# Attention scores of a head's two maps: hi-by-hi products on halves of the array's rows, crossed products in one pass per map

## The chip, the cores and the metric

The kernel runs on one core of a Trainium2 chip, in one launch. The metric is device time in microseconds (us). The kernel before takes 486.52 us, the median of three runs (486.24 to 486.82). Engine names are those of the profile: PE is the matmul engine and PEld its weight loads, DVE, ACT and POOL are the vector, scalar and GpSimd engines, and SP issues most of the DMAs.

## The reference

The layer takes 1,024 tokens of width 1,024, puts 16 learned meta tokens in front, and runs two mixers side by side on one input projection: differential attention with 4 heads, and a gated linear recurrence. Both have a SiLU gate; one output projection, the residual and a final norm follow. The part that matters here is the attention. A head has two maps, each with its own queries and keys of width 64, and the difference of their two softmaxes weighs the values:

```
scores = jnp.einsum('bqhmd,bkhmd->bhmqk', qb, kb).astype(jnp.float32) * scale
mask = cid[s:e, None] >= cid[None, :kend]
scores = jnp.where(mask[None, None, None], scores, -jnp.inf)
p = jax.nn.softmax(scores, axis=-1)
w = p[:, :, 0] - lam * p[:, :, 1]
outs.append(jnp.einsum('bhqk,bkhd->bqhd', w.astype(vb.dtype), vb))
```

Queries are taken in blocks of 128 and see all keys up to the end of their last chunk of 64, so block i (0 to 7) has 16 + 128(i+1) keys.

## The kernel before, in words

All matrix products keep float32 accuracy by splitting: an operand is stored as a high part (hi) and the rest (lo), and a product is summed from hi by hi, hi by lo and lo by hi. The projections do it with three f32 passes. The scores do it in f16: for each of the 8 maps, the scratch tensors `q_d` and `k_d` in DRAM hold 128 rows, rows 0 to 63 the hi part of the 64 features and rows 64 to 127 the lo part.

The program runs through the projections one weight group after the other (x of the recurrence, K, Q, the attention gate, the recurrence's gate), up to about 247 us. `run_group` walks a group's four blocks of eight k-steps and starts, by the table `PL`, the fetching and splitting of the next group's weights. In the last group, the recurrence's gate, each finished block goes to `g_evac`, in which DVE reads it out of PSUM into the tile `gl`; after block number `LK` it also issues the loads of K and of the first query tile on SP's queue.

Then `attend` goes through 32 steps, one head of one query tile each: tiles 3, 7, 6, 5, 4, 2, 1, 0, so that steps 0 to 3 are tile 3, 4 to 7 tile 7, and so on to steps 28 to 31 for tile 0, with four more steps for what still trails. One step holds, in the order in which every engine gets it:

- the transposes of the hi half of the weights of the head three steps back (`trans(0)`, PSUM tile `pt`, copied by ACT into `wT`);
- `scores` of the head's map 0;
- a first third of the step's fill units. These are pieces of other matrix work (V's projection `psv`, the recurrence's part of the output `psol`, the attention's part `psoa`), some six matmuls each; the table `MF` tells for each step how many are due;
- `combine` of the head before: the two maps' exponentials become one weight matrix;
- a second third of the fill, the transposes of the lo half (`trans(1)`), `scores` of map 1, and the rest of the fill;
- `halve`, which splits the weights of the head before into f16 hi and lo, and `weigh`, the product of weights and values of the head four steps back (PSUM tile `O`).

`scores` writes one map's scores into a PSUM buffer `pss`, by two full passes over K: the first has q as stored (hi over lo) against K as stored, which gives hi by hi and lo by lo; the second has q with its halves exchanged (`q[:, 1]`, loaded so by `load_q`), which gives the two crossed products. Then DVE reduces the buffer (it scales, masks, writes the tile `e` and keeps the extreme in `mx`; the profile's CUSTOM_DVE_ANT_0), and ACT takes the exponential. There are two wide buffers `pss` of two banks each, the same two that the projection groups before use for their blocks, in turn; a buffer can be written again when its reader is done. From tile 2 on, where 400 columns or fewer are needed, the two are of one bank.

All instructions pass through one helper line, L77, so the profile's rows tell operations apart by their tiles, not their lines. In DMA rows, L218 is the load of a projection's weights (`wraw`), L774 that of K, L757 a store of the attention gate.

Of the kernel before, what the change touches and what calls it, by code (L numbers as in the profile page):

```python
# [34 lines left out]
G_XL, G_GL, G_Q, G_K, G_GA, G_V = range(6)  # L35
# [63 lines left out]
def hybrid_layer_kernel(ctx: ExitStack, tc: tile.TileContext, xT, x, meta, w6, nwT,  # L99
# [5 lines left out]
    dma = nc.sync.dma_start  # L105
# [26 lines left out]
    def score_banks():  # L132
        if narrow:
            return narrow[0].tile([P, 512], F32, tag="S1", name="pss")
        return two_banks()
# [635 lines left out]
    def load_k():  # L771
        for m in range(0, NMAP, 2):
            kt = slot("K", [P, 2, T], F16, name="kst")
            dma(kt, qk_d[G_K][m:m + 2].rearrange("m p t -> p m t"))  # L774
            K.extend([kt[:, 0, :], kt[:, 1, :]])

    QT = {}
# [23 lines left out]
            load_k()  # L801
            load_q(tiles[0])

    LK = 1


    rsv = cst([P, NT + 1], name="rsv")
# [70 lines left out]
    def scores(i, h, a):  # L878


        d = st[i]
        n, k0, q, m = d["n"], d["k0"], QT[i], 2 * h + a
        ps = score_banks()
        for j in range(2):
            for s0 in range(0, n - k0, 512):
                s1 = min(s0 + 512, n - k0)
                PE.matmul(ps[:, s0:s1], q[:, j, m, :], K[m][:, k0 + s0:k0 + s1], start=(j == 0), stop=(j == 1))
        e = slot("work", [P, T], name="e")
        mx = d["mx"][:, a, h:h + 1]
        if k0:  # L890
            A.copy(e[:, 0:NM], d["sme"][:, m, :])
        V.tensor_tensor_reduce(out=e[:, k0:n], in0=ps[:, 0:n - k0], in1=mask[:, T - n + k0:], op0=OP.add, op1=OP.min,
                               scale=nesc, scalar=d["m2"][:, m:m + 1] if k0 else -NEG, accum_out=mx)
        if a == 0:
            A.activation(mx, mx, AF.Identity, bias=lnsw)
        A.activation(e[:, 0:n], e[:, 0:n], AF.Exp, scale=-1.0, bias=mx, accum_out=d["sm"][:, a, h:h + 1])
        d["e"][h, a] = e
# [248 lines left out]

    filled = [0]

    MF = [8, 5, 10, 5, 2, 5, 5, 4, 1, 3, 3, 0, 1, 1, 0, 2, 1, 2, 3, 0, 1, 2, 2, 0, 2, 3, 1, 2, 1, 3, 1, 3, 2, 3, 0, 0]

    def at_least(n):
        while fill and filled[0] < n:
# [36 lines left out]
    def attend():  # L1189
# [12 lines left out]
        for s in range(NS + TL + 1):  # L1202
            cur = order[s] if s < NS else None
            com = order[s - 1] if 0 <= s - 1 < NS else None
            tra = order[s - TL] if 0 <= s - TL < NS else None
            filled[0] = 0
            if cur and max(tiles[tiles.index(cur[0]):]) <= PB and not narrow:

                wide.close()
                narrow.append(ctx.enter_context(tc.tile_pool(name="psS1", bufs=NB_[0], space=bass.MemoryType.PSUM)))  # L1210
                narrow.append(ctx.enter_context(tc.tile_pool(name="psF", bufs=NB_[1], space=bass.MemoryType.PSUM)))
            trans(0)
            if cur:
                i, h = cur
                if h == 0:
                    begin(i)
                scores(i, h, 0)
                if h == QH and i in after:
                    load_q(after[i])
            at_least((MF[s] + 2) // 3)  # L1220
            if com:
                combine(*com)
            at_least((2 * MF[s] + 2) // 3)
            trans(1)
            if cur:
                scores(i, h, 1)
                pace()
            at_least(MF[s])
            if com:
                halve(*com)  # L1230
            if avq:
                weigh(*avq[0])
            if tra:
                avq.append(tra)
            while len(backlog) > BL:
                fill_one()
            yield
# [93 lines left out]
```

## Time and profile before

| | |
|---|---|
| median of three runs | 486.52 us |
| the profiled execution | 486.57 us |
| its span, first to last instruction | 484.8 us |
| mean granted PE clock | 0.996 |
| score matmuls (`pss` from `kst` and `qt`) | 208, 247.4 to 442.3 us |
| step 0 starts | 247.4 us |
| the last output products start | 465.3 us |

A PE row of the timeline is a group of matmuls merged, with its start, the time from the first start to the last end, and the count. A matmul's recorded end is modelled and holds its latency, so what one costs in a sequence is read from the distance between starts, not from its length. A weight load (PEld) overlaps the matmul before it. The page's shares of the chain say what the end of the program was waiting for, step by step back from the end. The form 128\*128 before a matmul's shape is rows by columns of the array in use: 16\*128 uses 16 rows.

### The profile page before, as it was taken

What the parts mean: (1) busy time and instruction counts of PE and PEld (TensorE: products, weight loads), DVE (VectorE), ACT (ScalarE), POOL (GpSimd) and SP (SyncE); (2) the same over time, 40 slices, a digit from 0 to 9 for tenths busy, and PEclk for the clock granted to TensorE, in tenths of its full rate; (3) what the DMA queues carried; (4) which work ended last, traced back from release to release, by engine and by line L of the source; (5) the groups of instructions that cost most, each with busy time, mean ns of one, the idle gap of its engine ahead of it and who ended that gap; (6) DMA issues with size and microseconds to landing.
All of it is one profiled execution on the core that took longest, in us unless ns stands there. A gap on an engine that the chain in (4) does not pass through costs nothing.

```text
span 484.8 us, 7748 instructions
## 1 busy us (share of the span) xinstructions
PE 466.2 (96%) x2844; PEld 375.4 (77%) x2844; DVE 364.3 (75%) x610; ACT 303.3 (63%) x592; POOL 126.1 (26%) x171
## 2 busy tenths in 40 slices
PE   6999999999999999999999999999988999999894
PEld 5996989988888888888877577777766778877783
DVE  5756987496799576974574477789999989898443
ACT  5687532663626838441583367698787877797733
POOL 0102202201010000000001044185142425365772
PEclk9999999999999999999999999999999999999998
DMA  7993221344023115239445124953943576315523
GB/s 243 394 398 124 89 89 31 80 121 120 23 65 88 44 43 174 87 124 346 141 139 187 45 61 138 265 172 91 275 110 91 131 193 153 121 32 197 195 88 130
DMA packets 50150, 68.33 MB, mean 141 GB/s; under 512 B 21008, under 2 KB 30128, under 8 KB 50112
## 3 DMA queue, kind: packets, MB, share of 16 engines
q1 hardware_dynamic: 38240, 55.21, 34.6%
q0 software_dynamic: 11872, 12.63, 10.7%
q8 instruction: 22, 0.36, 0.3%
q14 instruction: 16, 0.13, 0.1%
HBM read 48.91 MB, written 18.91 MB: 140 GB/s over the span
## 4 chain that ended last, share of the span: by engine, by line
PE 87%; DVE 5%; ACT 3%; issue 2%; DMA 1%; POOL 0%; POOLq 0%; ACTq 0%; SPq 0%
PE pss L77 42%; PE psv L77 9%; PE psol L77 7%; PE psoa L77 7%; PE ps L77 6%; PE psx L77 5%; PE O L77 4%; DVE e L77 3%; PE psg L77 2%; PE pt L77 2%; DMA res<-res_d 1%; DVE w L77 1%; PE psmr L77 1%; PE pa L77 1%; ACT wT L77 1%
## 5 line engine op out<-in xcount | busy, mean ns | idle before, releaser
L77 PE MATMUL pss<-xs,w 128*128 128x512 f32 (+1 forms) x720 | 142.4, 345 | 4.3 <-ACT xs L77 4.3
L77 PEld LDWEIGHTS pss<-xs,w 128*128 128x128 f32 x720 | 120.4, 190 | 24.5 <-ACT xs L77 4.3
L77 ACT ACTIVATE e<-e,mx 128x528 f32<-128x528 f32 (+7 forms) x64 | 50.5, 790 | 27.4 <-DVE mx L77 26.1
L77 PE MATMUL psv<-w,xs 128*128 128x512 f32 x192 | 48.4, 402 | 0.2 <-DVE v L77 0.2
L77 DVE CUSTOM_DVE_ANT_0 e<-pss,mask,nesc 128x528 f32<-128x528 f32 (+6 forms) x56 | 42.6, 761 | 7.7 <-PE pss L77 6.5
L77 PE MATMUL pss<-w,xs 128*128 128x512 f32 x192 | 46.0, 394 | 0.0
L77 PE MATMUL psol<-woh,lr 128*128 128x512 f32 x128 | 42.8, 415 | 1.9 <-ACT wT L77 1.9
L77 DVE TENSOR_TENSOR w<-wraw,w 128x512 fp32r<-128x512 f32 (+2 forms) x49 | 31.7, 669 | 16.2 <-ACT w L77 16.0
L77 PE MATMUL pss<-kst,qt 128*128 128x512 f16 (+3 forms) x208 | 42.6, 318 | 0.7 <-DVE mx L77 0.7
L77 PEld LDWEIGHTS psv<-w,xs 128*128 128x128 f32 x192 | 35.3, 188 | 10.0 <-issue 0.8
L77 PEld LDWEIGHTS pss<-w,xs 128*128 128x128 f32 x192 | 35.7, 188 | 7.9
L77 PE MATMUL psoa<-woh,at 128*128 128x512 f32 (+1 forms) x136 | 41.6, 389 | 0.2 <-ACT psoa L77 0.2
L77 ACT COPY wT<-pt 128x1024 f16<-128x1024 f16 (+5 forms) x48 | 37.6, 784 | 1.0 <-PE pt L77 0.8
L77 DVE SCALAR_TENSOR_TENSOR e<-e,mx 128x528 f32<-128x528 f32 (+7 forms) x32 | 35.0, 1095 | 1.1
L77 ACT ACTIVATE w<-wraw 128x512 fp32r<-128x512 f32 x47 | 28.5, 619 | 9.7 <-DMA wraw<-in_w_dram 9.2
L77 PE MATMUL ps<-xs,w 128*128 128x512 f32 x120 | 34.4, 394 | 0.0
L77 PEld LDWEIGHTS <-wT 128*128 128x128 f16 x432 | 25.6, 98 | 6.6 <-issue 2.7
L77 PE MATMUL O<-v,wT 128*128 128x128 f16 x432 | 29.4, 219 | 1.3 <-ACT wT L77 1.3
L77 DVE TENSOR_TENSOR w<-e,w 128x528 f16<-128x528 f32 (+7 forms) x32 | 28.9, 904 | 0.9
L77 PEld LDWEIGHTS psol<-woh,lr 128*128 128x128 f32 x128 | 22.9, 188 | 8.6 <-ACT wT L77 3.2
L77 DVE RECIPROCAL a<-a 128x208 f32<-128x208 f32 x20 | 27.8, 1423 | 0.0
L77 PEld LDWEIGHTS psoa<-woh,at 128*128 128x128 f32 x136 | 24.1, 188 | 4.5 <-ACT psoa L77 0.4
(197 smaller groups left out, 838.4 us busy)
## 6 DMA issues: line engine op xcount, KB each, us to landing
wraw<-in_w_dram SPq DMA_DIRECT2D x47, 256.0 KB, 3.9
xt<-in_x_dram SPq DMA_DIRECT2D x8, 512.0 KB, 7.0
woraw<-in_w_out_dram SPq DMA_DIRECT2D x8, 512.0 KB, 3.5
xres<-in_x_dram SPq DMA_DIRECT2D x8, 512.0 KB, 4.9
lr<-lru_d POOLq DMA_DIRECT2D x8, 512.0 KB, 5.1
res_d<-xres SPq DMA_DIRECT2D x8, 512.0 KB, 3.1
res<-res_d SPq DMA_DIRECT2D x8, 512.0 KB, 4.4
out_dram<-res SPq DMA_DIRECT2D x7, 512.0 KB, 2.9
```

Of the source, the lines that this page charges most:

```text
L77: return f(*a, **k)
```

## The change

K is stored differently on the chip: for odd maps the halves are exchanged, lo in rows 0 to 63 and hi in rows 64 to 127. This takes three DMAs for two maps in place of one, twelve in all, and they are issued after block 0 of the last group in place of block 1.

A step writes the scores of both maps at its start. First come hi by hi: map 0 on rows 0 to 63 (hi of q as stored, hi of K) and map 1 on rows 64 to 127 (hi of the exchanged q, hi of the exchanged K), into the two buffers `pss`, in turn for each cut of up to 512 columns. Then each map gets one pass on all rows that adds its two crossed products: map 0 with the exchanged q, map 1 with q as stored against the exchanged K. The product lo by lo, which the first pass held before, is not computed any more. DVE's reduction and ACT's exponential of map 1 follow those of map 0 at once.

Six entries of `MF` change by one, with the same sum.

```diff
@@ load_k
             kt = slot("K", [P, 2, T], F16, name="kst")
-            dma(kt, qk_d[G_K][m:m + 2].rearrange("m p t -> p m t"))
+            dma(kt[:, 0], qk_d[G_K][m])
+
+            dma(kt[0:64, 1], qk_d[G_K][m + 1, 64:128])
+            dma(kt[64:128, 1], qk_d[G_K][m + 1, 0:64])
             K.extend([kt[:, 0, :], kt[:, 1, :]])
...
-    LK = 1
+    LK = 0
@@ scores
-        ps = score_banks()
-        for j in range(2):
-            for s0 in range(0, n - k0, 512):
-                s1 = min(s0 + 512, n - k0)
-                PE.matmul(ps[:, s0:s1], q[:, j, m, :], K[m][:, k0 + s0:k0 + s1], start=(j == 0), stop=(j == 1))
+        cuts = [(s0, min(s0 + 512, n - k0)) for s0 in range(0, n - k0, 512)]
+        if a == 0:
+
+            d["ps"] = [score_banks() for _ in range(2)]
+            for s0, s1 in cuts:
+                for b in range(2):
+                    r = slice(64 * b, 64 * b + 64)
+                    PE.matmul(d["ps"][b][:, s0:s1], q[r, b, m + b, :], K[m + b][r, k0 + s0:k0 + s1], start=True, stop=False)
+        ps = d["ps"][a]
+        for s0, s1 in cuts:
+            PE.matmul(ps[:, s0:s1], q[:, 1 - a, m, :], K[m][:, k0 + s0:k0 + s1], start=False, stop=True)
...
-    MF = [8, 5, 10, 5, 2, 5, 5, 4, 1, 3, 3, 0, 1, 1, 0, 2, 1, 2, 3, 0, 1, 2, 2, 0, 2, 3, 1, 2, 1, 3, 1, 3, 2, 3, 0, 0]
+    MF = [8, 5, 10, 5, 2, 5, 5, 4, 2, 3, 2, 0, 1, 1, 0, 2, 1, 2, 3, 0, 1, 2, 1, 1, 2, 3, 1, 2, 1, 3, 1, 3, 1, 3, 1, 0]
@@ attend
                 scores(i, h, 0)
+                scores(i, h, 1)
+                pace()
                 if h == QH and i in after:
                     load_q(after[i])
...
             trans(1)
-            if cur:
-                scores(i, h, 1)
-                pace()
             at_least(MF[s])
```

The order of instructions at three places. On PE, the start of step 0, from the last matmul of the projection groups on (a number at a tile's name tells its buffers apart, `pss_2090` and `pss_2098` being the last block's). Before:

```order
L77 MATMUL pss_2090<-xs_374,w_1867 128x512
L77 LDWEIGHTS qt_2009
L77 MATMUL pss_2187<-kst_2001,qt_2009 128x512
L77 LDWEIGHTS qt_2009
L77 MATMUL pss_2187<-kst_2001,qt_2009 128x16
L77 LDWEIGHTS qt_2009
L77 MATMUL pss_2187<-kst_2001,qt_2009 128x512
L77 LDWEIGHTS qt_2009
L77 MATMUL pss_2187<-kst_2001,qt_2009 128x16
L77 MATMUL psv_2200<-w_2041,xs_93 128x512
```

With the change:

```order
L77 MATMUL pss_2098<-xs_374,w_1867 128x512
L77 LDWEIGHTS qt_1952
L77 MATMUL pss_2195<-kst_1936,qt_1952 128x512
L77 LDWEIGHTS qt_1952
L77 MATMUL pss_2196<-kst_1936,qt_1952 128x512
L77 LDWEIGHTS qt_1952
L77 MATMUL pss_2195<-kst_1936,qt_1952 128x16
L77 LDWEIGHTS qt_1952
L77 MATMUL pss_2196<-kst_1936,qt_1952 128x16
L77 LDWEIGHTS qt_1952
L77 MATMUL pss_2195<-kst_1936,qt_1952 128x512
```

Two buffers are written in turn from the second score on, where before only one was touched before the V products.

On DVE at the same place, from the reading of the last gate block on (ISA with `e` as output is the reduction of a map's scores). Before:

```order
L77 TENSOR_TENSOR gl<-pss,Rb 128x1024
L77 ISA e,mx_2184<-pss,mask,nesc 128x528
L77 ISA mx_2184 128x1
L77 TENSOR_TENSOR gl<-gl,gls 128x1024
L77 TENSOR_TENSOR gl<-gl,gate_1675 128x1024
L77 TENSOR_TENSOR yl<-gl,yh 128x1024
L77 ISA e,mx_2184<-pss,mask,nesc 128x528
```

With the change:

```order
L77 TENSOR_TENSOR gl<-pss,Rb 128x1024
L77 ISA e,mx_2192<-pss,mask,nesc 128x528
L77 ISA mx_2192 128x1
L77 ISA e,mx_2192<-pss,mask,nesc 128x528
L77 ISA mx_2192 128x1
L77 TENSOR_TENSOR gl<-gl,gls 128x1024
L77 TENSOR_TENSOR gl<-gl,gate_1675 128x1024
```

The second map's reduction stands right behind the first one's, ahead of the gate's products.

On PE in step 34, from the last transposes of tile 0 on. Before:

```order
L77 MATMUL pt<-idh,w_4721 128x128
L77 LDWEIGHTS w_4721
L77 MATMUL pt<-idh,w_4721 128x128
L77 LDWEIGHTS wT
L77 MATMUL O<-v,wT 128x128
```

With the change:

```order
L77 MATMUL pt<-idh,w_4729 128x128
L77 MATMUL psoa<-woh,at 128x512 x2
L77 MATMUL psoa<-wol,at 128x512
L77 MATMUL psoa<-woh,at 128x512 x2
L77 MATMUL psoa<-wol,at 128x512
L77 LDWEIGHTS wT
L77 MATMUL O<-v,wT 128x128
```

One fill unit, six products of the output, now stands between the transposes and the products on `O`.

## The prediction

> **What bounds the kernel now.** I read the page's busy time and chain first, then busy time by stretch, then the timeline of the attention part. The page's lines of busy time and the chain's shares by engine:
>
> ```profile
> span 484.8 us, 7748 instructions
> ...
> PE 466.2 (96%) x2844; PEld 375.4 (77%) x2844; DVE 364.3 (75%) x610; ACT 303.3 (63%) x592; POOL 126.1 (26%) x171
> ...
> PE 87%; DVE 5%; ACT 3%; issue 2%; DMA 1%; POOL 0%; POOLq 0%; ACTq 0%; SPq 0%
> ```
>
> PE is busy 96% of the span and holds 87% of the chain. The change touches only what runs after 247 us. By stretch there (columns: busy us and count of PE, weight load, DVE, ACT, POOL; granted clock; DMA share; GB/s):
>
> ```profile
> 247.00:326.00 79.00, 78.78 (x454) 56.69 (x453) 53.84 (x90) 50.22 (x90) 24.72 (x19) 1.00 0.45 137
> 326.00:400.00 74.00, 68.94 (x653) 53.31 (x651) 70.19 (x126) 59.66 (x129) 26.45 (x37) 1.00 0.58 151
> 400.00:443.00 43.00, 42.65 (x332) 33.97 (x331) 39.19 (x111) 34.96 (x105) 21.89 (x32) 1.00 0.38 111
> 443.00:474.00 31.00, 29.72 (x153) 23.65 (x152) 15.71 (x39) 17.38 (x50) 22.29 (x26) 1.00 0.47 165
> ```
>
> From 247 to 326 (steps 0 to 7: tiles 3 and 7) PE idles 0.2 of 79 us, so each PE microsecond there is one of the kernel. From 326 to 400 (tiles 6, 5, 4) DVE is fuller, 70.2 of 74 against 68.9: both nearly bind, and a PE gain may stay there. From 400 to 474 PE binds again, with 1.6 us idle. After 474 only the last tile's ending is left, which the change leaves alone.
>
> **Fewer passes: -7.9 us.** The score matmuls by shape:
>
> ```profile
> L77 PE MATMUL pss<-kst,qt 128*128 128x512 f16 x96 | 30.3, 380 | 0.0
> ...
> L77 PE MATMUL pss<-kst,qt 128*128 128x400 f16 x32 | 9.2, 332 | 0.7 <-DVE mx L77 0.7
> L77 PE MATMUL pss<-kst,qt 128*128 128x272 f16 x32 | 7.6, 279 | 0.0
> ...
> L77 PE MATMUL pss<-kst,qt 128*128 128x144 f16 x32 | 6.0, 227 | 0.1
> ...
> L77 PE MATMUL pss<-kst,qt 128*128 128x16 f16 x16 | 2.7, 172 | 0.0
> ```
>
> Two pieces of the chain (start, length, instructions), four scores of 512 columns and the product after them:
>
> ```profile
> 295.58 0.86 PE pss L77 x4
> 296.44 0.69 PE psv L77 x3
> ```
>
> The mean of one (380 ns) holds its latency; in a row four take 0.86 us, 0.215 each, or 0.42 ns per column. All scores are 96x512 + 32x400 + 32x272 + 32x144 + 16x16 = 75,520 columns. Before, a head's two maps take four full passes. After, two half-row passes run side by side as one, and two crossed passes follow: three. A quarter of the columns, 18,880 x 0.42 ns = 7.9 us, goes; 2.6 us of it falls in steps 0 to 7, 4.0 between 326 and 400, 1.4 later. If the halves don't run together, this term is 0: these are its two ends. I take the full gain, since the pair reads different rows and writes different PSUM buffers. [...]
>
> **A toll at each change of rows: +5.0 us.** Now every one of the 32 steps goes from 128 rows to 64 and back, 64 changes; the kernel before does it at two small places in the whole program. The nearest rows, three places of PE's timeline:
>
> ```profile
> 256.32 0.64 PE L77 MATMUL pss<-kst,qt 128*128 128x512 f16 x4
> 256.81 1.64 PE L77 MATMUL psv<-w,xs 128*128 128x512 f32 x6
> 258.29 0.28 PE L77 MATMUL psf<-f,ones 128*128 128x8 f32 x2
> 258.43 1.63 PE L77 MATMUL psv<-w,xs 128*128 128x512 f32 x6
> ...
> 276.96 0.64 PE L77 MATMUL pss<-kst,qt 128*128 128x512 f16 x4
> 277.53 0.38 PE L77 MATMUL psvr<-rsv,sl 16*128 16x1 f32 x2
> ...
> 46.23 0.39 PE L77 MATMUL psx<-dgm,ones 16*128 16x16 f32 x2
> 46.55 0.52 PE L77 MATMUL pss<-xs,w 128*128 128x264 f32 x2
> ```
>
> The same four scores are followed after 0.49 us by a product on all rows, after 0.57 by one on 16: 0.08 for going in. A tiny f32 pair on all rows is left after 0.14, the one on 16 rows after 0.32: 0.18, in which slower f32 weight loads are held too. So a change costs from 0 (if halves are not treated so) to 0.18; I take 0.08, the f16 row, since scores are f16. The first one hides in the wait below: 63 x 0.08 = 5.0 us. [...]
>
> **A new wait in step 0: +3.1 us.** The two wide PSUM buffers of the scores are also those of the last two blocks before. The timeline there:
>
> ```profile
> 247.40 0.64 PE L77 MATMUL pss<-kst,qt 128*128 128x512 f16 x4
> ...
> 247.89 8.58 PE L77 MATMUL psv<-w,xs 128*128 128x512 f32 x36
> ...
> 248.71 0.69 DVE L77 TENSOR_TENSOR w<-wraw,w 128x512 fp32r<-128x512 f32 x1 [0.53 <-ACT w L77]
> 249.32 1.22 DVE L77 TENSOR_TENSOR gl<-pss,Rb 128x1024 f32<-128x1024 f32 x1
> 250.46 0.76 DVE L77 CUSTOM_DVE_ANT_0 e<-pss,mask,nesc 128x528 f32<-128x528 f32 x1
> ```
>
> Before, map 0 takes the free buffer at 247.40, and 8.6 us of V products stand ahead of map 1's scores at 256.32; by then DVE has long read the last block of the gate (gl, 249.32 to 250.54) out of the other buffer. Now PE's second instruction of step 0 writes that other buffer. It waits till 250.54, and the 36 V products queued behind it wait too: 250.54 - 247.40 = 3.1 us, with nothing on PE but one half pass. DVE can't be earlier: ahead of gl stand weight splits that wait for ACT. DVE has its two reductions from about 251.4, and the gate's next operations move behind them, by 1.3 us; what they feed is first loaded at 303:
>
> ```profile
> L1040 POOL DMA_DIRECT2D lr<-lru_d x8: 892/948/974, 303.1 to 401.6; - x8
> ```
>
> The bounds are 0 (if DVE came sooner) and 3.3.
>
> **Cover at the end: -1.3 us.** In the last steps PE waits once, for the copy of the last weights:
>
> ```profile
> 452.30 0.33 PE L77 MATMUL O<-v,wT 128*128 128x128 f16 x3
> 452.47 0.22 PE L77 MATMUL ptm<-idh,wm 128*128 128x128 f16 x1
> 453.96 0.34 PE L77 MATMUL O<-v,wT 128*128 128x128 f16 x3 [1.28 <-ACT wT L77]
> ...
> 453.56 0.35 ACT L77 COPY wT<-pt 128x256 f16<-128x256 f16 x1
> ```
>
> The new table moves six output products from step 32 into step 34, between the last transposes and these. Their 1.4 us (six products) cover the 1.28; bounds 0 and 1.3. The table's other moves (one unit each between steps 8 and 10, 22 and 23) keep the count of products and I cost them at 0: they lie in the stretch where DVE binds or swap neighbours. One small wait, V products for DVE in step 1, loses 0.2 since eight scores now stand ahead of it:
>
> ```profile
> 261.56 0.73 PE L77 MATMUL psv<-w,xs 128*128 128x512 f32 x2 [0.22 <-DVE v L77]
> ```
>
> **The K loads: 0.** Twelve DMAs in place of four, issued one block earlier and ahead of two weight loads on SP's queue:
>
> ```profile
> 213.39 0.90 SPq L218 DMA_DIRECT2D wraw<-in_w_dram  x2
> ...
> 214.66 1.96 SPq L774 DMA_DIRECT2D kst<-k_d  x4
> ...
> 222.31 13.15 SPq L218 DMA_DIRECT2D wraw<-in_w_dram  x6
> ...
> 231.31 0.63 ACT L77 ACTIVATE w<-wraw 128x512 fp32r<-128x512 f32 x1
> ```
>
> The page's row of these loads (count, KB, us to landing):
>
> ```profile
> wraw<-in_w_dram SPq DMA_DIRECT2D x47, 256.0 KB, 3.9
> ```
>
> At 0.49 us an issue twelve take 5.9 us, 3.9 more. The two weight loads, issued before at 213.39, now go out at about 225 and land 3.9 us later, against a first use at 231.31. So 2 us of cover are left; without it ACT's splits, and with them gl and the wait above, would slip by what is missing. K itself is first needed at 247.40.
>
> **Map 1's reduction moved up: 0.** DVE now does both reductions of a step, then the combining of the head before, which had to wait for map 1's exponential; that has now a whole step. Queued behind the second reduction are only that combining and the f16 halves, and the transposes that read them come two steps later. In the tight stretch this may win back part of DVE's 3.8 idle us or, if PE comes late to both maps, cost as much; I take 0.
>
> **Sum.** -7.9 + 5.0 + 3.1 - 1.3 - 0.2 = -1.3 us. The profiled execution took 486.57 us (span 484.8 and 1.8 around it), the median is 486.52: 485.3.
>
> **The rivals.**
> 1. *No toll for halves.* Then -6.3; but of the 4.0 us saved between 326 and 400 DVE, with 3.8 idle, lets perhaps half through: 482.3. For it: the tolls shown are of 16 rows and f32 operands, none of 64. Against it: it was paid both in and out.
> 2. *The toll is heavier and eats the gain* (slower). At a change of 0.13, midway between 0.08 and 0.18, 63 changes cost 8.2 us: 488.5. It decides from (7.9 + 1.5 - 3.1) / 63 = 0.10 on. [...] Against it: f16 loads are short.
> 3. *DVE keeps the middle.* What PE saves from 326 to 400, 4.0 less 24 x 0.08 = 2.1 us, only becomes waiting: 487.4. DVE's 70.2 of 74 speaks for it, its 3.8 idle against.
> 4. *The halves don't run together*, so the change doesn't do what it says: +7.9, of which PE's 5.1 idle us in the middle may hide a little: 492.
>
> **How the numbers follow.** My forecast (483.8 to 486.8) gets 0.36, rival 1 0.29, rival 2 0.14, rival 3 0.12, rival 4 0.09. The predicted time is 485.3. The range 480.8 to 489.6 takes in rivals 1 to 3 with their spread and leaves out most of rival 4 and a full gain without toll. About 0.2% (1.0 us) is what a measurement tells from no change. Faster: 0.6 of my forecast and nearly all of rival 1, 0.50. Slower: 0.1 of my forecast, rivals 2 and 4 and half of 3, 0.33. Within 0.2%: 0.17.
>
> **What would show it.** Half-row scores on 64 rows that start in pairs a few tens of ns apart show the passes saved; 0.215 us between the two shows rival 4. The distance from a pair's last matmul to the first crossed one, less its own columns, is the toll. PE idle of about 3 us at 247, ended by DVE's gl, shows the new wait; no idle before the last products on O at about 453 shows the cover. PE's busy time from 326 to 400 falling with DVE's unchanged shows rival 3. I am wrong if step 0 doesn't wait, or if the toll is outside 0 to 0.13.

## The result, and the profile after

The changed kernel takes 491.65 us, the median of three runs (490.58 to 491.92), against 486.52 before. The ratio is 1.010, with a 95% interval from 1.0075 to 1.0125: slower by 1%, where 485.3 us and a small gain had been forecast, and outside the range.

The page of the changed kernel, its span, busy times, chain and the group of the scores:

```profile
span 490.1 us, 7746 instructions
...
PE 466.5 (95%) x2844; PEld 371.5 (76%) x2844; DVE 359.6 (73%) x610; ACT 302.6 (62%) x592; POOL 124.3 (25%) x171
...
PE 73%; DVE 8%; DMA 5%; issue 5%; ACT 5%; POOL 2%; SPq 0%; POOLq 0%; DVEq 0%; ACTq 0%
...
L77 PE MATMUL pss<-kst,qt 64*128 64x512 f16 (+4 forms) x208 | 34.7, 323 | 4.0 <-DVE gl L77 2.7
```

PE is busy as long as before (466.5 us against 466.2), so the saved passes do not show in the sum, and its share of the chain has fallen from 87% to 73%: other engines now hold it up. Busy time by stretch, the columns as in the prediction:

```profile
247.00:251.00 4.00, 1.34 (x7) 0.32 (x6) 2.52 (x3) 2.11 (x6) 0.00 (x0) 0.94 0.30 103
251.00:254.00 3.00, 3.00 (x10) 2.15 (x9) 2.61 (x6) 2.15 (x4) 0.00 (x0) 0.52 0.00 0
247.00:326.00 79.00, 75.63 (x426) 53.92 (x425) 49.80 (x86) 47.01 (x86) 18.60 (x17) 0.98 0.38 114
326.00:400.00 74.00, 67.37 (x644) 49.83 (x643) 65.85 (x118) 57.70 (x118) 30.61 (x38) 1.00 0.61 166
400.00:443.00 43.00, 43.00 (x340) 32.92 (x339) 37.95 (x110) 35.90 (x107) 19.98 (x29) 1.00 0.36 103
443.00:474.00 31.00, 29.43 (x160) 23.19 (x158) 19.04 (x46) 18.06 (x57) 21.29 (x27) 1.00 0.50 174
```

Two things are new. PE idles 3.4 us in the first 79, and from 251 to 254 the granted clock is 0.52 with PE busy all the time. PE's timeline at that place, and DVE's:

```profile
247.26 0.39 PE L77 MATMUL pss<-kst,qt 64*128 64x512 f16 x1
250.31 1.46 PE L77 MATMUL pss<-kst,qt 64*128 64x512 f16 x7 [2.66 <-DVE gl L77]
251.62 6.62 PE L77 MATMUL psv<-w,xs 128*128 128x512 f32 x23
...
249.04 1.22 DVE L77 TENSOR_TENSOR gl<-pss,Rb 128x1024 f32<-128x1024 f32 x1
```

The second score of step 0 comes 3.05 us after the first, released by DVE's `gl`, as forecast. Then three microseconds run at half the clock, which costs 3 x 0.48 = 1.4 us more; that had not been forecast. All that PE waits for from 326 to 400, in the changed kernel (us in total, times, longest), and then before:

```profile
PE pa L77 <- POOL o L77: 2.8, 3, 1.7
PE psol L77 <- ACT wT L77: 1.5, 2, 0.9
PE pss L77 <- DVE mx L77: 1.4, 2, 0.8
PE pt L77 <- DVE mx L77: 1.0, 1, 1.0
```

```profile
PE psol L77 <- ACT wT L77: 1.9, 3, 1.0
PE pa L77 <- POOL o L77: 1.5, 1, 1.5
...
```

6.7 us of waits stand against 5.0 (the three rows left out have 0.7, 0.7 and 0.2): what the array saves there (1.6 us of busy time) is waited away again.

Where the time goes is easiest to see from the start of each step (its first score in the trace), as the difference to the same step before. The table holds some of the runs that are told of below as well; all numbers are us, and "median" is the whole time. A row comes from one execution. The seven kernels with fill first are alike up to step 0, and there their first scores lie up to 0.7 us apart, so a few tenths between two rows mean little.

| kernel | step 1 | 8 | 16 | 20 | 24 | 31 | span | median |
|---|---|---|---|---|---|---|---|---|
| the change | +4.3 | +3.5 | +4.2 | +3.9 | +4.5 | +4.6 | +5.3 | 491.65 |
| fill first (step 0's wait away) | -0.4 | -1.3 | +0.1 | -0.3 | +4.1 | +4.2 | +4.5 | 490.93 |
| the same with the old table | -0.2 | -1.1 | +2.4 | +0.7 | +2.9 | +3.6 | +6.6 | 493.35 |
| new order, full passes, fill first | -0.5 | -0.7 | -1.2 | -2.6 | +2.0 | +1.2 | +5.5 | 492.02 |
| change in steps 0 to 7 alone, fill first | -0.1 | -1.1 | -1.7 | -1.7 | -1.7 | -1.8 | -1.4 | 485.13 |
| the same with step 0's wait | +4.7 | +3.8 | +3.8 | +3.8 | +3.8 | +3.7 | +4.0 | 490.92 |
| change in steps 0 to 19, fill first | 0.0 | -0.9 | -1.0 | -1.0 | +0.2 | -0.5 | +2.4 | 488.74 |
| the same, full passes in steps 8 to 19 | +0.1 | -0.9 | -0.7 | -1.1 | +0.1 | -0.5 | +2.4 | 488.85 |
| the same (halves), old table throughout | -0.1 | -1.1 | +3.7 | +1.9 | +2.6 | +2.6 | +5.7 | 491.72 |

### The profile page after: what moved, and what is told of

The parts are those of the page before. It is cut to its first block, busy times and chain, and to the rows that moved or that the text cites. A ratio compares the mean times of both kernels' runs of the same rounds, so it can differ in the third digit from the quotient of the medians.

```text
span 490.1 us, 7746 instructions
## 1 busy us (share of the span) xinstructions
PE 466.5 (95%) x2844; PEld 371.5 (76%) x2844; DVE 359.6 (73%) x610; ACT 302.6 (62%) x592; POOL 124.3 (25%) x171
## 3 DMA queue, kind: packets, MB, share of 16 engines
q1 hardware_dynamic: 38368, 55.21, 34.7%
## 4 chain that ended last, share of the span: by engine, by line
PE 73%; DVE 8%; DMA 5%; issue 5%; ACT 5%; POOL 2%; SPq 0%; POOLq 0%; DVEq 0%; ACTq 0%
PE pss L77 35%; PE psv L77 9%; PE psoa L77 7%; PE ps L77 6%; PE psol L77 5%; DVE e L77 4%; PE O L77 3%; DMA wraw<-in_w_dram 3%; PE psg L77 2%; PE psx L77 2%; PE pt L77 2%; ACT w L77 2%; DMA xt<-in_x_dram 1%; DVE w L77 1%; DMA res_d<-xres 1%
## 5 line engine op out<-in xcount | busy, mean ns | idle before, releaser
L77 DVE CUSTOM_DVE_ANT_0 e<-pss,mask,nesc 128x528 f32<-128x528 f32 (+6 forms) x56 | 40.6, 763 | 6.2 <-PE pss L77 4.8
L77 PEld LDWEIGHTS psv<-w,xs 128*128 128x128 f32 x192 | 36.4, 193 | 9.8 <-issue 0.8
L77 PE MATMUL pss<-kst,qt 64*128 64x512 f16 (+4 forms) x208 | 34.7, 323 | 4.0 <-DVE gl L77 2.7
L77 ACT ACTIVATE w<-wraw 128x512 fp32r<-128x512 f32 x47 | 28.6, 620 | 10.8 <-DMA wraw<-in_w_dram 10.3
L77 ACT ACTIVATE mx<-mx,lnsw 128x1 f32<-128x1 f32 x32 | 9.4, 295 | 31.0 <-DVE mx L77 30.9
L77 DVE SCALAR_TENSOR_TENSOR e<-e,mx 128x528 f32<-128x528 f32 (+7 forms) x32 | 27.3, 853 | 1.1
```

Source lines behind the costliest of these rows:

```text
L77: return f(*a, **k)
```

## The experiments

Three causes were open: the wait in step 0, the halves with their toll, and the new order (both maps written and reduced at the step's start). Every kernel below computes the whole result.

One thing holds for all of them. The program keeps a model of its own of when each engine is done (`Clock`), and it issues the operations that finish a tile, among them the four transposes `pa` of the attention's output, when the model says that their input is ready. So an edit that shifts the modelled times also moves some of these operations to other places in the queues, and many kernels below differ in more than the edit shown. The pair with halves or full passes in steps 8 to 19 is the cleanest: DVE, ACT and POOL have the same order in both. The kernel with the change in steps 0 to 7 alone and its twin with step 0's wait differ by a few operations of steps 0, 8 and 9 only.

### The wait in step 0 taken away

The wait can go if the other buffer is read before step 0's scores come to it, so three units of fill (V products) are put ahead of them; a second kernel puts one unit there.

```diff
             if cur:
                 i, h = cur
+                if s == 0:
+                    at_least(3)
                 if h == 0:
                     begin(i)
                 scores(i, h, 0)
```

> The changed kernel, but in step 0 the first three fill units (18 V products, 4.2 us by 0.23 each) stand ahead of the scores, so that the last gate block is read before the second buffer is asked for. Theory 1 (the wait at the start of step 0 and the slower clock after it cost 4.3 of the 5.1 us): no PE idle at 247, granted clock 1.00 there, 487.2 us (486.4 to 488.0). Rival (what the changed kernel loses is lost evenly over the steps, by the changes of rows): the gap at 247 goes but the time is won back nowhere, 490 to 491.7.

> As the run with three units ahead, with one unit (6 products, 1.4 us) ahead of the scores: PE still waits about 1.6 us for the buffer. Theory 1 with the clock as a part of its own (waiting 3.05 us costs 3.05, and some 1.4 more as the clock halves for 3 us): the shorter wait leaves the clock at 1.00, 1.6 us above the run with three units, 488.8. Rival (the clock falls after any wait there): 3 us above it, 490.2.

With three units: 490.93 us, ratio to before 1.0085 (1.0068 to 1.0103). With one unit: 492.69 us, 1.0123 (1.0108 to 1.0138), above both expected values. There PE still waits 1.3 us for `gl`, the clock stays at 1.00, and step 1 starts 1.7 us sooner than in the change, but a stall of 2.2 us comes at step 23. In the first, the wait is gone, the clock is not cut there (1.00 from 247 to 262), and at step 8 the kernel is 1.3 us ahead of before and 4.8 us ahead of the change. But at the end only 0.7 us of the 4.8 is left. 4.0 us go in one place, between the starts of steps 22 and 24. PE there, then ACT, then DVE:

```profile
406.94 0.61 PE L77 MATMUL pa<-idf,o 128*128 128x128 f32 x4
409.85 0.49 PE L77 MATMUL pt<-idh,w 128*128 128x128 f16 x6 [2.31 <-ACT wT L77]
...
407.56 0.29 ACT L77 ACTIVATE mx<-mx,lnsw 128x1 f32<-128x1 f32 x1 [1.70 <-DVE mx L77]
407.89 0.63 ACT L77 ACTIVATE e<-e,mx 128x400 f32<-128x400 f32 x1
...
408.52 0.61 ACT L77 ACTIVATE e<-e,mx 128x400 f32<-128x400 f32 x1
...
409.13 0.67 ACT L77 COPY wT<-pt 128x640 f16<-128x640 f16 x1
...
406.40 0.58 DVE L77 TENSOR_TENSOR w<-e,w 128x400 f16<-128x400 f32 x1
406.89 0.63 DVE L77 CUSTOM_DVE_ANT_0 e<-pss,mask,nesc 128x400 f32<-128x400 f32 x1
```

The transposes `pt` wait for a PSUM bank that ACT's copy `wT` empties. The copy now stands behind both exponentials of the step, the first of these waits 1.70 us for DVE's reduction, and DVE comes to that only when it has split the weights of the head before. Before the change one exponential stands there, not two. That alone doesn't make the stall, though. The change has both exponentials ahead of this copy as well, and ACT waits 1.61 us for DVE there (up to 411.31), but PE doesn't wait. What differs is `pa`: `pt`, `ptm` (the transpose of the meta tokens' weights) and `pa` take three banks in turn, so with `pa` ahead the next `pt` needs the bank of the `pt` at 405.75 again. In the change `pa` comes one step later, at 413.88, and a bank is free. The two other kernels with this stall, one unit ahead and the order alone below (2.2 and 3.0 us), have `pa` ahead of it too; no run moves `pa` by itself. After the stall the clock is cut again (0.54, the third number from the end):

```profile
411.00:414.00 3.00, 3.00 (x15) 2.15 (x14) 2.86 (x9) 1.87 (x6) 1.95 (x3) 0.54 0.00 0
```

So the wait in step 0 is real, but taking it away brings a stall elsewhere.

### The table, and the order without halves

Two kernels on the base of fill first: one with the table `MF` of before, one with the new order but two full passes a map (so lo by lo is computed again, as before the change).

```diff
+    MF = [..., 1, 3, 3, 0, ..., 2, 2, 0, 2, ..., 2, 3, 0, 0]   # the old table
```

```diff
-            for s0, s1 in cuts:
-                for b in range(2):
-                    r = slice(64 * b, 64 * b + 64)
-                    PE.matmul(d["ps"][b][:, s0:s1], q[r, b, m + b, :], K[m + b][r, k0 + s0:k0 + s1], start=True, stop=False)
         ps = d["ps"][a]
+        for s0, s1 in cuts:
+            PE.matmul(ps[:, s0:s1], q[:, a, m, :], K[m][:, k0 + s0:k0 + s1], start=True, stop=False)
```

> Three units ahead in step 0, and the table of fill units as it was in the kernel before. If the new table's cover at the end is worth the 1.3 us that I forecast: 1.3 slower than the run with the new table. If its six products only move the wait (the changed kernel still shows 1.9 us of waits for O): within 0.5 us of it.

> Three units ahead in step 0, both maps at the start of a step, but each by two full passes of 128 rows as in the kernel before: no halves, no changes of rows (the product lo by lo is computed again). PE's work in it is 7.9 us more in passes and 6.0 less in changes of rows than with halves, so if PE binds throughout it is 1.9 slower than the run with halves. If the middle (tiles 6, 5, 4) is held by other things than PE, it loses only what steps 0 to 7 and 20 to 31 say: 1.0 slower in the first, 1.0 faster in the last, so the same within 0.5.

The old table: 493.35 us, 1.013 (1.0114 to 1.0145), 2.4 us above fill first. The order alone: 492.02 us, 1.0121 (1.0095 to 1.0148), 5.3 us slower than before without a half pass, a toll or step 0's wait. It is as slow as the change, within the intervals. Its losses lie late: it is 2.6 us ahead of before at step 20, loses 4.6 us by step 24 and 4.3 more behind step 31. So a loss of this size needs no halves; the order makes one, with its table and with the places that `pa` and its like then get. From step 1 to step 8 the halves show their worth: 0.95 us won with them, 0.18 with full passes, so 0.8 us. With the old table one unit less stands in step 8, and a stall of 2.9 us comes in step 9; by step 31 that kernel is level with fill first again, and it loses its 2.4 us behind it (3.0 there, against 0.3).

### The toll, measured by doubling it

The pair and its crossed passes are written cut by cut, so that each of steps 0 to 19, where a map needs two cuts, changes rows four times and not twice.

```diff
             for s0, s1 in cuts:
                 for b in range(2):
                     r = slice(64 * b, 64 * b + 64)
                     PE.matmul(d["ps"][b][:, s0:s1], q[r, b, m + b, :], K[m + b][r, k0 + s0:k0 + s1], start=True, stop=False)
+                for b in range(2):
+                    PE.matmul(d["ps"][b][:, s0:s1], q[:, 1 - b, m + b, :], K[m + b][:, k0 + s0:k0 + s1], start=False, stop=True)
         ps = d["ps"][a]
-        for s0, s1 in cuts:
-            PE.matmul(ps[:, s0:s1], q[:, 1 - a, m, :], K[m][:, k0 + s0:k0 + s1], start=False, stop=True)
```

> Three units ahead in step 0; hi by hi and crossed products of one cut of 512 columns before those of the next, so that every step of tiles 3 to 4 with two cuts (steps 0 to 19) changes rows four times in place of twice. If a change costs 0.095 us (the changed kernel's starts: 0.151 against 0.056 into the pair, 0.308 against 0.215 out of it), each step of tile 7 is 0.2 longer on PE, and by step 8 it is 1.4 to 1.6 us behind the run without (7 steps by 0.2), the whole 1 to 4 slower as far as the middle lets it show. If changes cost nothing, step 8 starts within 0.2 us of that run.

It takes 492.13 us, 1.0116 (1.0101 to 1.0131), 1.2 us above fill first. Up to step 8, where the array sets the time, the sixteen extra changes cost 1.77 us (step 8 starts 0.47 behind before, against 1.30 ahead), 0.11 each. The changed kernel's trace has it directly, at the last step:

```profile
443.21 0.28 PE L77 MATMUL pt<-idh,w 128*128 128x128 f16 x2
443.42 0.47 PE L77 MATMUL pss<-kst,qt 64*128 64x144 f16 x4
443.69 0.71 PE L77 MATMUL psoa<-woh,at 128*128 128x512 f32 x2
```

Two transposes on all rows take 0.11 us in a row; the scores on 64 rows come after 0.21, so 0.10 for going in. The pair and the two crossed passes of 144 columns take 0.06 and 0.12 us; the next product comes after 0.27, so 0.09 for going out.

### Where in the step the second map's work stands

Four kernels keep fill first and the halves and have one edit each. The first puts the crossed pass, reduction and exponential of map 1 back behind the lo transposes, with the new table, and a second the same with the old table. The third leaves the new order and moves the lo transposes ahead of the scores, so that ACT's copies stand ahead of both exponentials. The fourth, run later, leaves the array's order new and puts back only DVE's and ACT's part, with the old table.

```diff
                 scores(i, h, 0)
-                scores(i, h, 1)
...
             trans(1)
+            if cur:
+                scores(i, h, 1)
+                pace()
```

```diff
             trans(0)
+            trans(1)
             if cur:
...
-            trans(1)
             at_least(MF[s])
```

> Three units ahead in step 0; hi by hi of both maps and the crossed products of map 0 at the start of a step, but map 1's crossed products, its reduction and exponential back where they were, after the lo transposes. Theory 2 (from step 8 on the loss is due to the order: ACT's copy of the lo transposes stands behind both exponentials, and PE waits for its PSUM bank): no wait of 2.5 us before step 24, and from step 8 on at least as fast as the kernel before, 484 to 486.5. Rival (halves or changes of rows cost it, not the order): as the run with both at the start, 490 to 492.

> As the run with map 1 late, with the table of fill units of the kernel before, whose order it then has save for the halves. Theory 2: the old table fits the old order, so 0 to 1.5 faster than with the new table, 483.5 to 486. If the table does nothing by itself, within 0.5 of it.

> Three units ahead in step 0; all scores written first as in the changed kernel, but the lo transposes stand ahead of them too, so that ACT copies both before the two exponentials. Theory 2: the banks come free early, 485.5 to 488. Rival (what hurts is that DVE does both reductions ahead of combine, not ACT's order): 490 or more, with DVE waits as in the changed kernel.

> Fill first, the table MF of before, and on the array the new order (the pair and both crossed passes at the step's start), but map 1's reduction on DVE and its exponential on ACT back behind the lo transposes, so that DVE and ACT have the order of before. Theory A2 (the place of map 1's reduction and exponential in the two queues is what makes w and wT late): no stall at step 23, and the halves' own balance is left, 18,880 columns x 0.42 ns = 7.9 us less, 63 changes of rows x 0.095 = 6.0 us more: 484.5 to 486.5 us. Theory E (the second score buffer is held from the step's start until map 1's reduction, so the next pair waits for DVE): 489 to 494 us, with waits of the scores on DVE's mx in many steps. The kernel with the crossed pass of map 1 late as well and the same table took 497.7 us.

Map 1 late: 503.61 us, 1.0348 (1.0329 to 1.0367); with the old table 497.74, 1.0236 (1.0199 to 1.0273). Lo transposes first: 491.0, 1.0097 (1.0081 to 1.0114), as fill first, where 485.5 to 488 had been the theory's range. The stall of 2.3 us at step 23 is gone there, but the transposes now wait 4.1 us for DVE's `w` in step 14, and the clock is cut behind that wait (0.50 from 369 to 372). Only DVE's and ACT's part late: 511.07, 1.0497 (1.0476 to 1.0518). The three late ones wait for one thing, here by the longest waits of PE from 247 us on, in the order of their naming:

```profile
PE pss L77 <- DVE mx L77: 13.6, 10, 2.3
```

```profile
PE pss L77 <- DVE mx L77: 13.8, 11, 2.8
```

```profile
PE pss L77 <- DVE mx L77: 17.9, 11, 5.5
```

Before, the scores wait for DVE's `mx` for 0.7 us in all. The pair writes both buffers at a step's start; if map 1 of the step before is reduced late, its buffer is still held. So the early reduction isn't a choice that the change could have left out: with two buffers, the pair on two halves of the rows asks for it. My theory that the place of map 1's reduction in the two queues makes the loss, and that putting it back would cure it, fell with 511 us; it had been stated with 484.5 to 486.5.

### Where in the program the loss is made

The change is kept for some tiles and all others get order and full passes of before. The kernels, all with fill first: halves and new order in steps 0 to 7 (tiles 3 and 7), with the old table; in steps 0 to 19, with the old table from step 20 on; the latter with full passes in steps 8 to 19; and in steps 0 to 19 with the old table throughout.

```diff
+    def halved(i):
+        return i in (3, 7)          # or i >= 3
...
+        if not halved(i):
+            ps = score_banks()
+            for j in range(2):
+                for s0, s1 in cuts:
+                    PE.matmul(ps[:, s0:s1], q[:, j, m, :], K[m][:, k0 + s0:k0 + s1], start=(j == 0), stop=(j == 1))
...
-                scores(i, h, 1)
+                if halved(i):
+                    scores(i, h, 1)
...
             trans(1)
+            if cur and not halved(i):
+                scores(i, h, 1)
```

> Fill first in step 0, halves and the new order in steps 0 to 7 alone (tiles 3 and 7), from step 8 on the order, the full passes and the table MF of before. Theory A (the array sets the time up to step 8, and the gain of the halves is real there; behind it DVE is busy 94 to 95% of the time in before, and the new order makes it late): the 1.3 us that the kernel with the fill first had won by the start of step 8 stay to the end, 486.5 - 1.3 = 485.2 us, between 484.7 and 485.9. Theory B (the loss is that of the narrow tiles' stall at step 23 alone): the same, 485.2. Theory C (the table MF is tuned so closely to the old starts that any shift costs more than it wins): 487 to 489, with the 1.3 us gone by step 16.

> As with the fill first, with halves and the new order in steps 0 to 19 (tiles 3, 7, 6, 5, 4), and the order, full passes and table of before from step 20 on. Theory B (the loss is the stall at step 23, 4.1 us, where the transposes wait for a bank that ACT empties late): step 20 starts 0.3 us ahead of before as with the fill first, the stall is gone, and the time is 486.0 to 487.0. Theory A (DVE keeps the middle, and the new order loses there too): the same start of step 20 or up to 2 us behind before, 486 to 488.5 us. Both: faster than the 490.9 us with the fill first by 3 us or more. If it stays above 489.5, neither holds and the loss is made before step 20.

> As the kernel with halves and new order in steps 0 to 19 and the rest of before (488.7 us), but in steps 8 to 19 two full passes a map in the new order: 9,216 columns x 0.42 ns = 3.9 us more on the array there, 24 changes of rows x 0.095 = 2.3 us less. Theories A2 and E (the array does not set the time there, the order does): within 1 us, 488 to 489.7 us. Theory F (the halves and their toll are the loss there): 486 to 487.5 us, as the loss of 3.6 us in these steps would be gone.

> Fill first, halves and new order in steps 0 to 19, the rest and the whole table MF of before; the only difference to the 488.7 us is the table (steps 8 and 10: 1 and 3 units in place of 2 and 2). Theory O (the new order makes the loss in steps 8 to 19): 488 to 489.5 us. Theory T (the order costs little there, step 20 started 1.0 us ahead of before; the rest was lost by units of fill that came at other places at steps 22 and in the tail): 485.3 to 487 us, without the two waits of psoa on ACT in the tail (1.9 us).

In steps 0 to 7 alone: **485.13 us, ratio 0.9963 (0.9949 to 0.9978)**, faster than before and than the change, as the theory had it (485.2). Step 8 starts 1.1 us ahead of before, step 16 and all behind it 1.7 us; the 0.6 between are from step 13, where PE's wait for POOL's `o` has shrunk from 1.5 us to 0.2. In steps 0 to 19: 488.74, 1.0041 (1.0028 to 1.0053). With full passes in steps 8 to 19: 488.85, 1.0041 (1.0025 to 1.0056). With the old table throughout: 491.72, 1.0101 (1.0084 to 1.0118).

The second and third of these agree in median and nearly in every step start, though the third has 3.9 us more of passes and 2.3 less of toll: in steps 8 to 19 the halves are worth nothing either way. Busy time there, with halves and then with full passes:

```profile
326.00:400.00 74.00, 67.67 (x657) 50.74 (x656) 66.44 (x124) 57.81 (x119) 27.84 (x35) 1.00 0.60 155
```

```profile
326.00:400.00 74.00, 69.01 (x658) 53.72 (x657) 66.83 (x124) 57.91 (x120) 27.78 (x35) 1.00 0.59 155
```

PE is busy 1.3 us less with the halves, step 20 starts no earlier for it, and DVE isn't full in either. With the old table throughout, one stall decides, in step 9, on PE's timeline:

```profile
333.82 1.00 PE L77 MATMUL O<-v,wT 128*128 128x128 f16 x15
337.76 1.01 PE L77 MATMUL pt<-idh,w 128*128 128x128 f16 x8 [2.94 <-DVE xres L77]
```

The six microseconds behind it, with a granted clock of 0.50:

```profile
337.00:343.00 6.00, 5.24 (x23) 3.23 (x23) 3.85 (x7) 2.04 (x4) 2.14 (x4) 0.50 0.99 279
```

2.9 us of waiting are followed by some 6 us of work at half the clock, 3 us lost once more. One unit of fill more in step 8 keeps this stall away, which the new table has; my theory that mixing the tables was what cost the 488.7 us fell. All three kernels with the new order in steps 0 to 19 lose another 3 us behind step 31; PE's waits for the banks of `psoa` rise from 0.2 to 1.9 us in each. In these three, in the order alone and in fill first with the old table, the program puts 54 output products between the last products on `O` and the last tile's `pa`, where before, the change, fill first and the change in steps 0 to 7 alone have 42. There `pa` comes 13.2 to 14.1 us behind those products, here 10.3 to 10.4. So this loss goes with where the program puts the last tile's operations; no run here moves them by themselves.

### Two more places for map 1's reduction

With the array's order new in steps 0 to 19, DVE's and ACT's part of map 1 late in all of these steps, or in steps 8 to 19 only; all of before from step 20 on.

```diff
             if halved(i):
-                scores(i, h, 1)
                 pace()
...
             trans(1)
-            if cur and not halved(i):
+            if cur:                       # or: if cur and i not in (3, 7)
                 scores(i, h, 1)
```

> The same in steps 0 to 19 (tiles 3, 7, 6, 5, 4), and order and full passes of before from step 20 on. Theory A2: 484 to 485.5 us, 3 us or more faster than with both reductions at the start of these steps (488.7). Theory E: 487 to 491 us.

> Both reductions at the start in steps 0 to 7, the array's order new with map 1's reduction late in steps 8 to 19, and all of before from step 20 on. Theory A2: 484 to 485.5 us, as the kernel with the late reductions in all of steps 0 to 19 or a little faster. Theory E: steps 0 to 7 gain 1.3 us as in the kernel with the change there alone, and steps 8 to 19 lose 2 to 4 us: 487 to 489 us.

507.71 us, 1.0422 (1.0399 to 1.0446), and 490.32 us, 1.0073 (1.0057 to 1.0089). In steps 8 to 19 alone, late reductions are 1.6 us worse than early ones (488.74), with 6.8 us of waits for `mx`. The first kernel differs from the second in steps 0 to 7 only, is 3.0 us behind it at step 8 and 17 at the end: one more sign that the loss behind step 8 hangs on how the steps before it end.

### Is it DVE's load?

Eight casts of `w` (tiles 6 and 5) go from DVE to ACT, in the kernel with fill first and in the kernel before.

```diff
-    PH = (7, 3)
+    PH = (7, 6, 5, 3)
```

> As with the fill first, and the eight casts of w (tiles 6 and 5; 0.57 to 0.65 us each on DVE) on ACT as copies, as tiles 7 and 3 have it already. Theory A (DVE keeps steps 8 to 19): 4.9 us less work on the fullest engine there and shorter waits for w, so 2 to 4 us faster than with the fill first, 487 to 489 us, and step 20 starts 2 us or more ahead of before. Theory B (the stall at step 23 alone): no change within 1 us, 490 to 491.9. Rival D (ACT's queue is what is late, since its copies of wT stand behind the exponentials): slower, 492 to 494 us, since ACT has 7 us more to do.

> The kernel before, with the same eight casts on ACT, and nothing else. Theory A (DVE keeps the middle of before already): 484 to 486 us, 0.5 to 2.5 us faster than before. Theory B: within 0.5 us of before. Rival D (ACT late): 488 to 490 us.

493.28 us, 1.0141 (1.0121 to 1.0161), and 491.27 us, 1.0104 (1.0083 to 1.0125): slower by 2.4 and 4.6 us, although ACT is the emptier engine (56.9 us busy against DVE's 65.7 of the 74 from 326 to 400 with fill first, 59.7 against 70.2 before). Two of the longest waits of the first:

```profile
PE pt L77 <- ACT wT L77: 3.2, 4, 1.6
PE psol L77 <- ACT wT L77: 2.5, 2, 1.9
```

The waits for ACT's copies `wT` grow, from 3.2 us in all with fill first (2.3 and 0.9) to 5.7. That points to how soon ACT comes to the copy that frees a bank, more than to how busy DVE is. The move also puts ACT between two of DVE's own operations on `w`, so it is no clean test of DVE's load by itself.

### The price of step 0's wait at the end

The fastest kernel (the change in steps 0 to 7) with the units of fill ahead of step 0 taken out again.

> The kernel with halves and new order in steps 0 to 7 alone (485.1 us), without the units of fill ahead of step 0's scores, so that the second score waits there for DVE's read of the buffer. If the wait and the halved clock behind it (4.6 us by step 1 in the traces) stay to the end where nothing else is moved: 485.1 + 4.6 = 489.7 us, between 489 and 490.3. If the waits further on in steps 8 to 19 take it up (they would be shorter, as DVE and ACT come less late): 486.5 to 488.5.

490.92 us, 1.0095 (1.008 to 1.011): 5.8 us more than with the fill first, 5.4 by the spans. All of it stays to the end, where almost nothing behind step 8 is moved. The wait is the same as in the change (2.7 us, ended by `gl`), and so is the clock behind it:

```profile
251.00:254.00 3.00, 3.00 (x12) 2.20 (x11) 2.51 (x5) 2.45 (x4) 0.00 (x0) 0.58 0.00 0
```

This kernel is as slow as the change itself (490.92 and 491.65, intervals that overlap), though it has the change in 8 of 32 steps only.

## Why the prediction was wrong, and where it was right

**Fewer passes, -7.9.** The halves do run together. In the changed kernel a pair of 512 columns is one row of the timeline:

```profile
293.69 0.39 PE L77 MATMUL pss<-kst,qt 64*128 64x512 f16 x2
```

Two matmuls, both over within 0.39 us; their starts lie 3 ns apart in the trace. Rival 4 is out. That they would run together I had taken without a run that showed it. But only what falls in steps 0 to 7 became time. From step 1 to step 8 the change wins 0.8 us on before, net of the toll, and the halves 0.8 on full passes; the terms gave about 1.3 there. The 4.0 us for 326 to 400 became waiting, as rival 3 had it. The clean pair shows it: in steps 8 to 19 halves and full passes give the same time (488.74 and 488.85). DVE wasn't full in that stretch (66.4 and 66.8 of 74 us in the pair, 65.85 in the change, against 70.19 before).

**The toll, +5.0.** Right in kind, 0.09 to 0.11 a change and not 0.08: about 6 us in all. That every change to 64 rows and back pays it was my estimate, from a place with 16 rows; the changed kernel's trace has 0.10 for going in and 0.09 for going out. What the array does in that time no run shows. A weight load of 128x128 has a mean of 98 ns in f16 and 188 in f32 in the kernel before, so f16 loads are short, as held against rival 2.

**The new wait in step 0, +3.1: the term that failed first.** Place, cause and length were right; the price was not. What the wait costs at the end, where little else is moved, is 5.4 to 5.8 us. I counted the wait alone. With the cut clock behind it 4.8 us are gone by step 1 (+4.7 against -0.1); some of the rest is a wait of 0.5 us for `psol` in step 9 that the kernel without step 0's wait doesn't have. Whether each execution has the cut isn't shown: the profiled one of the change has a mean granted clock of 0.992, the two others 0.996, at 491.65 and 490.58 us. With 5.5 in place of 3.1 the sum is +1.1, about 487.7 us. The sum had no term for the clock. The traces of the two kernels with this wait of 2.7 us have it cut behind it, to 0.52 and 0.58 from 251 to 254.

**"Map 1's reduction moved up: 0": the term that failed second.** I saw that DVE's order changes and that later consumers have slack, and missed ACT, whose copies of `wT` now stand behind two exponentials, and the three PSUM banks which these copies free. The order with full passes costs 5.3 us, 4.6 of them between steps 20 and 24, where the stall on such a bank is, and 4.3 behind step 31. But the order is only a part of that cause: both losses come with a `pa` at another place than in the kernels without them. How much of the change's own loss is the order's stays open. Without step 0's wait, going from steps 0 to 7 to all steps, with the new table, costs 5.8 us (490.93 against 485.13). Of these some 1.6 lie in step 15, behind a cut clock that the same two waits did not bring in another kernel, and 4.0 at the stall. With the wait it costs 0.7 (491.65 against 490.92): that profile has neither, and its clock is 1.00 from 326 to 474.

**Cover at the end, -1.3: not got.** In place of one wait of 1.28 the products on `O` have three in the changed kernel, and behind the start of step 31 it loses 0.8 us on before:

```profile
PE O L77 <- ACT mT L77: 0.6, 1, 0.6
PE O L77 <- ACT o L77: 0.5, 1, 0.5
PE O L77 <- ACT wT L77: 0.5, 1, 0.5
```

**The K loads, 0: right.** `gl` starts at 249.04, before at 249.32; nothing ahead of it came late.

By the runs, the change in steps 0 to 7 with its wait makes 4.5 of the 5.1 us (490.92 against 486.39 in its own comparison): 5.8 lost by the wait, 1.3 won by the rest. What comes behind step 8 adds 0.7, which the intervals don't tell from nothing, where 5.3 - 48 x 0.08 + 1.3 = 2.8 us of gain had been forecast. This share-out is one of two. Counted from the other end, the change without the wait loses 4.2 us already (490.93 against 486.71), and the wait adds 0.9, where it costs 5.8 in the kernel with the change in steps 0 to 7. The prices don't add up, because one kernel's stalls and cut clocks are not the other's; why the change met those it met isn't shown. Most of the slower side's chance lay with a heavier toll and serial halves, and it was neither. Rival 3, a gain that only becomes waiting, was right from 326 to 400 and had 0.12.

## What to carry to other kernels

A wait on the array has two prices, its length and the clock that it may cut afterwards: give a stall of 2 to 3 us up to twice its length (here 2.7 us cost 4.8 by step 1, and 2.9 us had 3 more lost behind them), and look for work to put ahead of it. Before an engine's work is moved up, list what stands behind it on each queue that it passes, above all the copies that free a bank or a buffer, since these can hold the array before any engine is full (with fill first for 2.3 us at step 23, DVE being busy 34.7 and ACT 32.9 of the 43 us from 400 to 443). Where a program places operations by a model of its own, compare the queues of the two kernels before a difference is put down to the edit: here one group of four transposes, a step earlier, went with a stall of 2.3 us. When a change helps only where the array sets the time, make it there alone: here the same edit in 8 of 32 steps, with three units of other work ahead of the first, turns +1.0% into -0.4%.

## What the runs showed of the hardware

Stalls of 2.3 to 2.9 us were followed by half the clock for some 3.4 us (the change, 0.94 from 247 to 251 and 0.52 from 251 to 254; fill first, 0.54 from 411 to 414 and 0.67 from 414 to 415) or 6 us (old table throughout, 0.50 from 337 to 343). A wait of 1.3 us in step 0, with one unit ahead, left it at 1.00. But a longer stall need not cut it either. With the lo transposes first, PE waited as long, here on its timeline:

```profile
328.78 1.44 PE L77 MATMUL pss<-kst,qt 64*128 64x512 f16 x8
333.19 0.66 PE L77 MATMUL pa<-idf,o 128*128 128x128 f32 x4 [2.98 <-POOL o L77]
```

The clock behind it stayed at 1.00:

```profile
333.00:337.00 4.00, 3.81 (x19) 3.20 (x20) 3.07 (x8) 3.69 (x7) 2.82 (x4) 1.00 0.07 26
```

And two kernels had the same two short waits at the same place, 0.58 and 0.91 us with 1.3 us of scores between them. On PE's timeline, with the change in all steps and fill first:

```profile
364.54 1.26 PE L77 MATMUL pss<-kst,qt 64*128 64x512 f16 x7 [0.58 <-DVE mx L77]
366.70 1.10 PE L77 MATMUL psol<-woh,lr 128*128 128x512 f32 x2 [0.91 <-ACT wT L77]
```

With the change in steps 0 to 19:

```profile
364.93 1.26 PE L77 MATMUL pss<-kst,qt 64*128 64x512 f16 x7 [0.58 <-DVE mx L77]
367.10 0.73 PE L77 MATMUL psol<-woh,lr 128*128 128x512 f32 x2 [0.91 <-ACT wT L77]
```

The clock behind them, in the same two kernels, is 0.50 and 1.00:

```profile
367.00:370.00 3.00, 3.00 (x8) 2.32 (x8) 2.93 (x8) 1.88 (x5) 0.21 (x1) 0.50 0.00 0
```

```profile
367.40:370.40 3.00, 3.00 (x20) 2.30 (x19) 2.93 (x8) 1.88 (x5) 0.21 (x1) 1.00 0.00 0
```

So equal waits had other ends, and one of 2.98 us had no cut behind it; what decides that isn't shown, and no run here moves a wait on purpose. The length of a stall alone did not give its price here, and the sum made ahead could not know the rest: the time with and without the cut are its bounds.
